# Gate tables of two expert blocks by scattered accumulating DMAs, and inverse roots on ScalarE, in a hybrid decoder block

## The chip, the cores and the metric

One core of one Trainium2 chip runs the whole kernel: one decoder layer over 1024 tokens. The metric is device time in microseconds of one launch (the slowest core, here the only one). Engine names follow the profile: PE is TensorE's matmul, PEld its weight load, DVE is VectorE, ACT is ScalarE, POOL is GpSimd, and SP issues most of the DMAs.

## The reference, cut to what matters

```python
h = rmsnorm(x, mix_norm);  zc = h @ w_in
o_dn = gated_deltanet(...)            # conv, l2norm of q and k, chunked recurrence, rmsnorm of o
o_sw = swa_sink_attention(...)        # window 128
x = x + concat(o_dn, o_sw) @ w_out
x = x + peer(rmsnorm(x, ffn_norm))    # below
gate = sigmoid(rmsnorm(x, ple_norm) @ ple_gate)
x = x + gate * (p @ ple_proj);  out = rmsnorm(x, final_norm)

def peer(h):                          # 8 heads, 128 x 128 product keys, 16384 experts
    sc = keys of both halves . query                    # (T, 8, 2, 128)
    top_s, top_i = top_k(sc, 16)
    best_s, best_pos = top_k(all 16 x 16 sums, 16)
    expert = top_i[0] * 128 + top_i[1] at best_pos      # (T, 8, 16)
    gates = softmax(best_s)
    act = gelu(h . u_tab[expert])
    return sum over heads and picks of gates * act * v_tab[expert]
```

A token picks 128 experts, 16 in each of 8 heads. The heads' picks may name the same expert; their gates then add up.

## The kernel before

The 1024 tokens are 8 blocks of 128. The work has three stages, written one behind the other; a list scheduler orders the instructions of each engine when the kernel is built, by its own times, and each engine then runs its list in order.

**Upstream** (`upstream`, from L325). `projected` multiplies p with its projection and stores the product (`pr` to the DRAM table `prd`). `project(0)` and `project(1)` each norm 4 blocks, transpose them (`hTh`, `hTl`), and multiply with w_in, first 12 column tiles `ct` (weights `wraw` from `in_wc_dram`), then the rest. Blocks then go in four groups of two: `mixers` runs DeltaNet (`deltanet`) and windowed attention (`swa`), `retrieve` the output projection (`x`, stored as `x1d`), the norm, the queries, the scores and the two top-k (`first_topk`, `topk`). `mixers(gi + 1)` stands ahead of `retrieve(gi)`, so both interleave. All matmuls of weight size are three products of high and low parts in fp32r (`mm3`).

**Gates.** Blocks 5, 6, 7 (`ABLK`) keep lists of expert numbers (`eidx`) and gates. Blocks 0 to 4 (`DBLK`) need a dense table of gates, expert by token: `topk` transposes the first and second half of each expert number and the gate into `tT`, and `gbuild` makes the table by matmul. For 4 tokens at a time DVE compares an iota with both halves (`o12`, shown as `o`), ACT scales one half by the gates, four matmuls multiply them (`bk_gm`), and ACT copies the result into `stage`; after 16 tokens SP stores 1 MB to the DRAM table `gd`:

```python
tt(o12, bc(bc(iota, 1, 4), 1, 2), bc(tT[:, 0:2, c0:c0 + 4], 3, P), ALU.is_equal)
for i in range(4):
    copy(o2[:, i], o2[:, i], scale=tT[:, 2, c0 + i:c0 + i + 1])
for i in range(4):
    mm(pg[:, i], o2[:, i], o1[:, i])
copy(stage[:, :, t0:t0 + 4], pg.rearrange("p t e -> p e t"))
```

That is 32 such steps per block, 160 in all.

**Dense** (`dense`, L918). For 128 chunks of 128 experts the hidden products of the 640 dense tokens are made in two parts of 320 columns (`bk_u`), ACT takes gelu (`ge`), DVE multiplies by the gates `Gt` loaded from `gd`, and ACT and DVE split the product in `wh` and `wl`; after each 4 chunks the products with v follow (`bk_y`, `bk_yp`). Beside it POOL gathers the rows of u and v for blocks 5 to 7 by indirect DMAs (`rows`, L852) and DVE takes dots and sums. **Final** (`final`, L1007) does the last gate and norm.

`rsqrt` (L152) is two POOL instructions, a multiply-add into `rs_v` and a power into `rs` (norms), `rq` (l2norm of q and k) or `ro` (DeltaNet's output). `swa` clears `kz` and `vz` on POOL for every block and copies v into `vz` there.

Of the kernel before, what the change touches and what calls it, by code (L numbers as in the profile page):

```python
# [6 lines left out]

# [3 lines left out]
I32 = mybir.dt.int32  # L11
# [18 lines left out]
DBLK = [0, 1, 2, 3, 4]  # L30
ABLK = [5, 6, 7]
# [14 lines left out]
def _consts():  # L46
    import numpy as np

    r = np.arange(P)
    parts = [np.eye(P), r[:, None] <= r[None, :], r[:, None] > r[None, :], np.ones((P, P)),  # L50
             np.broadcast_to(r[None, :], (P, P)), r[None, :] > r[:, None]]
    for l in range(7):
        s = 1 << l
        same = (r[:, None] // (2 * s)) == (r[None, :] // (2 * s))
        low = same & (r[:, None] % (2 * s) >= s) & (r[None, :] % (2 * s) < s)
        parts.append(low if l == 0 else low.T[:, r % (2 * s) >= s])
    sel = np.zeros((P, 8 + 50 + 16 + 16 + 16))
    sel[:, :8] = (500000.0 ** (-np.arange(0, 16, 2) / 16)).astype(np.float32)
    widths = [16 // (a + 1) for a in range(16)]
    starts = np.concatenate([[0], np.cumsum(widths)[:-1]])  # L60
    sel[:, 58:74] = starts
# [6 lines left out]
def block_kernel(ctx: ExitStack, tc, I, out, dbg=None):  # L68
# [47 lines left out]
    G.memset(mhalf, -0.5)  # L116
    early = ExitStack()
# [7 lines left out]
    negt = c2.tile([P, 1], F32, name="negt")  # L125

    def load_consts():
        nc.sync.dma_start(ident, I["consts"][:, 0:P])
        nc.sync.dma_start(cst, I["consts"][:, P:])
        V.tensor_copy(sel_b.rearrange("p s a h -> p (s a) h"), bc(sel[:, 58:106], 2, 8))  # L130
        V.memset(negt, NEG)

# [14 lines left out]
    gd = dr.tile([NE // GC, P, NT // TB, GC, TB], F32, name="gd")  # L147

    eidx = cp.tile([P, len(UBLK), P], I32, name="eidx")
    gate_a = cp.tile([P, len(UBLK), P], F32, name="gate_a")  # L150

    def rsqrt(pool, dst, src, scale, n):  # L152
        v = pool.tile([P, n], F32, tag=f"rsv{n}", name="rs_v", bufs=2)
        G.tensor_scalar(v, src, scale, EPS, op0=ALU.mult, op1=ALU.add)  # L154
        G.tensor_tensor(dst, v, mhalf[:, 0:n], ALU.pow)  # L155
# [65 lines left out]
    def project(hf, es):  # L221
# [103 lines left out]
    def upstream():  # L325
        with early as em:
# [37 lines left out]
    def mixing(dn):  # L364
        sink = row(c2, "sinks", 8)
        state = {}
# [14 lines left out]
    def retrieving(lt, es):  # L381
# [14 lines left out]
        def retrieve(gi):  # L396
# [62 lines left out]
            for bi, b in enumerate(grp):  # L459
                topk(lt, bg, b, tv[bi], tiu[bi])  # L460
                if b in HBLK:
                    pools["job"] = half_job()
                tick(2.0)

# [200 lines left out]
    def swa(dn, state, b, zc_d, cos, sin, sink, mTh, mTl, cols):  # L665
# [85 lines left out]
    def topk(tk, bg, b, v, iu):  # L751
# [52 lines left out]
        ga = gate_a[:, UBLK.index(b)] if b in UBLK else flat[:, 2 * P:3 * P]  # L804
# [9 lines left out]
        if b in ABLK:  # L814
            return
# [13 lines left out]
    slots = {}  # L829

    def gbuild(bg, b):
        tT = slots[b]
        for tb in range(P // TB):
# [13 lines left out]
            nc.sync.dma_start(gd[:, :, BBLK.index(b) * (P // TB) + tb].rearrange("g p c t -> p g (c t)"),  # L847
# [64 lines left out]
    def tick(us):  # L912
        credit[0] += us * RATE
        n = int(credit[0])
        credit[0] -= n
        advance(n)

    def dense(xB):  # L918
        with ExitStack() as es:
# [12 lines left out]
            nparts = (NU + 511) // 512  # L932
            width = (NU // nparts + TB - 1) // TB * TB
            parts = [(n0, min(width, NU - n0)) for n0 in range(0, NU, width)]
# [26 lines left out]
            for cg in range(NE // GC):  # L961
                Gt = ap.tile([P, NT // TB, GC, TB], F32, tag="Gt", name="Gt", bufs=1)
                nc.sync.dma_start(Gt, gd[cg])
                vs, ws = [], []
                for ci in range(GC):
# [10 lines left out]
                    for n0, n in parts:  # L976
# [6 lines left out]
                        g3 = ge.rearrange("p (t k) -> p t k", k=TB)  # L983
                        m0 = NH + n0
                        tt(g3, g3, Gt[:, m0 // TB:(m0 + n) // TB, ci, :], ALU.mult)
# [76 lines left out]
    upstream()  # L1062
    pools["gp"] = ctx.enter_context(tc.tile_pool(name="gp", bufs=GBUF, side="right", reuse_waits="tile"))
# [64 lines left out]
```

## Time and profile before

| | |
|---|---|
| median of 3 runs | 3049.43 us (3043.96 to 3054.33) |
| the profiled execution | 3050.88 us, of which the span from first to last instruction is 3049.1 us |
| busy, PE / DVE / ACT / POOL | 2938.0 / 2504.2 / 1234.5 / 1067.8 us |
| first matmul of the dense stage | 1124.7 us after the span's start |
| granted TensorE clock, mean | 0.984 |

Matmuls are pipelined, so a busy PE is not PE at its peak. In a row of the timeline "x3" is three instructions merged; the first number is the start, the second how long they took together.

### The profile page before, as it was taken

What the parts mean: (1) busy time and instruction counts of PE and PEld (TensorE: products, weight loads), DVE (VectorE), ACT (ScalarE), POOL (GpSimd) and SP (SyncE); (2) the same over time, 40 slices, a digit from 0 to 9 for tenths busy, and PEclk for the clock granted to TensorE, in tenths of its full rate; (3) what the DMA queues carried; (4) which work ended last, traced back from release to release, by engine and by line L of the source; (5) the groups of instructions that cost most, each with busy time, mean ns of one, the idle gap of its engine ahead of it and who ended that gap; (6) DMA issues with size and microseconds to landing.
All of it is one profiled execution on the core that took longest, in us unless ns stands there. A gap on an engine that the chain in (4) does not pass through costs nothing. (4 is left out here: it accounts for less than half of the span.)

```text
span 3049.1 us, 49772 instructions
## 1 busy us (share of the span) xinstructions
PE 2938.0 (96%) x18287; PEld 2689.7 (88%) x18287; DVE 2504.2 (82%) x5023; ACT 1234.5 (40%) x2761; POOL 1067.8 (35%) x901
## 2 busy tenths in 40 slices
PE   7999999999998879999999999999999999999998
PEld 5888999999998778989889989999899999998977
DVE  5658635998999879989799889888898898798884
ACT  5567634488777653222223223223222232222232
POOL 0000000000000002655465555555555665556531
PEclk9999999999999899999999999999999999999999
DMA  6569666689879895999899989999999898899962
GB/s 233 143 230 364 201 204 223 225 231 255 230 220 275 229 301 193 358 347 328 288 351 349 342 323 338 338 323 338 339 332 336 317 364 314 306 345 335 325 227 84
DMA packets 449812, 869.24 MB, mean 285 GB/s; under 512 B 193440, under 2 KB 235680, under 8 KB 445216
## 3 DMA queue, kind: packets, MB, share of 16 engines
q1 hardware_dynamic: 338976, 463.37, 46.3%
q0 software_dynamic: 110592, 402.70, 36.5%
q8 instruction: 143, 2.34, 0.3%
q14 instruction: 101, 0.83, 0.1%
HBM read 766.34 MB, written 99.61 MB: 284 GB/s over the span
## 5 line engine op out<-in xcount | busy, mean ns | idle before, releaser
L134 PE MATMUL bk_u<-hT,uh 128*128 128x320 f32 x4096 | 912.7, 310 | 11.9 <-DMA hT<-h2Td 8.4
L134 PEld LDWEIGHTS bk_u<-hT,uh 128*128 128x128 f32 x4096 | 693.5, 188 | 28.3 <-DMA hT<-h2Td 8.8
L852 POOL DMA_INDIRECT rows<-in_u_dram,eidx x384 | 497.6, 1296 | 553.4 <-DVE dots L862 292.4
L134 PE MATMUL bk_u<-hT,ul 128*128 128x320 f32 x2048 | 633.6, 309 | 0.0
L852 POOL DMA_INDIRECT rows<-in_v_dram,eidx x384 | 498.5, 1298 | 365.1 <-DVE acc L82 291.0
L82 DVE SCALAR_TENSOR_TENSOR acc<-rows,dots,acc 128x1024 f32<-128x1024 f32 x384 | 491.5, 1280 | 19.1 <-DMA rows<-in_v_dram,eidx 12.3
L862 DVE CUSTOM_DVE_ANT_0 rows<-rows,h2n 128x1024 f32<-128x1024 f32 x384 | 457.8, 1219 | 18.3 <-DMA rows<-in_u_dram,eidx 17.4
L982 ACT ACTIVATE ge<-bk_u 128x320 f32<-128x320 f32 x256 | 109.7, 430 | 691.0 <-PE bk_u L134 659.4
L134 PEld LDWEIGHTS bk_u<-hT,ul 128*128 128x128 f32 x2048 | 385.1, 188 | 3.7
L134 PE MATMUL bk_y<-vh,wh 128*128 128x512 f32 x768 | 299.7, 391 | 2.9 <-DVE xB L79 2.9
L134 PE MATMUL bk_y<-vl,wh 128*128 128x512 f32 x768 | 300.9, 393 | 0.0
L134 PE MATMUL bk_y<-vh,wl 128*128 128x512 f32 x768 | 299.0, 394 | 0.0
L76 ACT ACTIVATE o<-o,tT 128x128 f32<-128x128 f32 x640 | 204.0, 392 | 55.6 <-DVE o L79 54.9
L76 ACT ACTIVATE wh<-ge 128x320 fp32r<-128x320 f32 x256 | 119.0, 469 | 262.9 <-DVE ge L79 246.3
L134 PE MATMUL bk_gm<-o 128*128 128x128 f32 x1280 | 200.8, 288 | 23.3 <-ACT o L76 13.4
L76 ACT ACTIVATE uh<-ur 128x1024 fp32r<-128x1024 f32 x128 | 135.4, 1058 | 188.1 <-PE bk_u L134 177.5
L134 PE MATMUL bk_s<-h,whi 128*128 128x256 f32 x1024 | 207.2, 295 | 3.7 <-ACT sc L76 1.9
L79 DVE TENSOR_TENSOR o<-cst,tT 128x1024 f32<-128x1024 f32 x160 | 193.7, 1214 | 18.4 <-PE bk_gm L134 17.5
L134 PE MATMUL bk_yp<-vh,wh 128*128 128x512 f32 x512 | 199.4, 394 | 7.4 <-ACT wh L76 7.4
L134 PEld LDWEIGHTS bk_gm<-o 128*128 128x128 f32 x1280 | 177.6, 197 | 29.7 <-ACT o L76 17.9
L134 PE MATMUL bk_yp<-vl,wh 128*128 128x512 f32 x512 | 199.4, 394 | 0.0
L79 DVE TENSOR_TENSOR ul<-ur,uh 128x1024 fp32r<-128x1024 f32 x128 | 156.3, 1221 | 45.2 <-ACT uh L76 45.1
(302 smaller groups left out, 5805.5 us busy)
## 6 DMA issues: line engine op xcount, KB each, us to landing
ur<-in_uT_dram SPq DMA_DIRECT2D x128, 512.0 KB, 6.9
vr<-in_v_dram SPq DMA_DIRECT2D x128, 512.0 KB, 6.7
gd<-stage SPq DMA_DIRECT2D x40, 1024.0 KB, 7.4
Gt<-gd SPq DMA_DIRECT2D x32, 1280.0 KB, 9.5
wlo<-wqc SPq DMA_DIRECT2D x128, 256.0 KB, 4.5
whi<-wqc SPq DMA_DIRECT2D x128, 256.0 KB, 4.5
whi<-woc SPq DMA_DIRECT2D x64, 256.0 KB, 4.5
wlo<-woc SPq DMA_DIRECT2D x64, 256.0 KB, 4.7
```

Of the source, the lines that this page charges most:

```text
L76: return S.activation(o, i, AF.Copy, **k)
L79: return V.tensor_tensor(o, a, b, op)
L82: return V.scalar_tensor_tensor(o, a, s, b, op0, op1, **k)
L134: PE.matmul(o, l, r, start=start, stop=stop)
L852: G.indirect_dma_start(out=r, out_offset=None, in_=tab, in_offset=bass.IndirectOffsetOnAxis(ap=eidx[:, u, s:s + 1], axis=0))
L862: held_back(V.tensor_tensor_reduce(out=r, in0=r, in1=h2n, op0=ALU.mult, op1=ALU.add, scale=1.0, scalar=0.0, accum_out=dots[:, s:s + 1]))
L982: S.activation(ge, pa, AF.Gelu_apprx_tanh)
```

## The change

Blocks 0 and 1 (`SBLK`) no longer go through `gbuild`. Their gates go into a DRAM table of their own, `gsd`, of 128 x 128 experts by 256 tokens, 4 bytes each, 16.8 MB. It is zeroed by 16 DMAs of 1 MB from an SBUF tile of zeros, two in the code of each of the first eight column tiles of `project(0)`. After the top-k of both blocks, `scattered` issues 256 indirect DMAs from POOL (8 heads x 2 blocks x 16 picks); each adds one gate of each of 128 tokens to its place in `gsd`. The 16 DMAs of a head and block wait for the 16 of the head before of that block. In the dense stage `Gs` is loaded from `gsd` and serves a first part of 256 columns, `Gt` a second one of 384. From the second mixers until the dense stage `rsqrt` is two ACT instructions, Ln and Exp, in place of the two on POOL. `kz` and `vz` are three persistent pairs, cleared once, and v is copied by ACT.

```diff
+SBLK = [0, 1]
+NS = len(SBLK) * 128
...
+        V.memset(zero, 0.0)
+        for i in range(len(SBLK)):
+            V.tensor_scalar(scol[:, i:i + 1], sel[:, 8:9], float(i * P), None, op0=ALU.add)
...
+    gsd = dr.tile([NE * P * NS, 1], F32, name="gsd")
+    lanes = dram_disjoint_views(gsd, 16 * len(SBLK))
...
     def rsqrt(pool, dst, src, scale, n):
         v = pool.tile([P, n], F32, tag=f"rsv{n}", name="rs_v", bufs=2)
+        if by_log[0]:
+            S.activation(v, src, AF.Ln, scale=scale, bias=eps)
+            S.activation(dst, v, AF.Exp, scale=-0.5)
+            return
         G.tensor_scalar(v, src, scale, EPS, op0=ALU.mult, op1=ALU.add)
         G.tensor_tensor(dst, v, mhalf[:, 0:n], ALU.pow)
...
+            if not hf and ct < 8:
+                for z in range(2 * ct, 2 * ct + 2):
+                    zf = gsd.rearrange("(z p n k) o -> z p n (k o)", z=16, p=P, k=512)[z]
+                    nc.sync.dma_start(zf, bc(zero, 1, zf.shape[1]))
...
                 retrieve, half_built = retrieving(lt, es)
+                by_log[0] = True
...
+            if any(b in SBLK for b in grp):
+                scattered([b for b in grp if b in SBLK])
...
-        kz = dn.tile([P, 2, P], F32, tag="kz", name="kz", bufs=3)
-        vz = dn.tile([P, 2, P], F32, tag="vz", name="vz", bufs=3)
-        G.memset(kz, 0.0)
-        G.memset(vz, 0.0)
+        kz, vz = state["z"][b % 3]
         copy(kz[0:64, 0], pk[0:64])
         copy(kz[64:128, 1], pk[64:128])
         for kv in range(2):
-            G.tensor_copy(vz[:, kv, 64 * kv:64 * kv + 64], qk[:, 10 + kv])
+            copy(vz[:, kv, 64 * kv:64 * kv + 64], qk[:, 10 + kv])
...
-        if b in ABLK:
+        if b in SBLK:
+            si = SBLK.index(b)
+            stt(i1, i1, 128.0, i2, ALU.mult, ALU.add)
+            V.tensor_scalar(sidx[:, si], i1, float(NS), scol[:, si:si + 1], op0=ALU.mult, op1=ALU.add)
+        if b in ABLK or b in SBLK:
             return
...
+    def scattered(blocks):
+        for h in range(8):
+            for b in blocks:
+                si = SBLK.index(b)
+                now = []
+                for k in range(16):
+                    s = h * 16 + k
+                    i = G.indirect_dma_start(
+                        out=lanes[16 * si + k], out_offset=bass.IndirectOffsetOnAxis(ap=sidx[:, si, s:s + 1], axis=0),
+                        in_=sgate[:, si, s:s + 1], in_offset=None, compute_op=ALU.add)
+                    for j in sent.get(b, ()):
+                        tc.add_manual_dep(i.ins, j.name,
...
+                    now.append(i.ins)
+                sent[b] = now
...
-            parts = [(n0, min(width, NU - n0)) for n0 in range(0, NU, width)]
+            parts = [(0, NS), (NS, NU - NS)]
...
+                Gs = ap.tile([P, GC, NS], F32, tag="Gs", name="Gs", bufs=1)
+                nc.sync.dma_start(Gs, gsd.rearrange("(g c p t) o -> g p c (t o)", c=GC, p=P, t=NS)[cg])
...
+                        if n0 == 0:
+                            tt(ge, ge, Gs[:, ci], ALU.mult)
+                        else:
+                            g3 = ge.rearrange("p (t k) -> p t k", k=TB)
+                            tt(g3, g3, Gt[:, :, ci, :], ALU.mult)
...
     upstream()
+    by_log[0] = False
```

Three places show how the order of the instructions moves. SP near the program's start, before the change (`xt` are blocks of x, `prd` the stores of the first product, `wraw` raw weights):

```order
L236 DMA xt<-in_x_dram 128x1024 x2
L202 DMA wraw<-in_wp_dram 128x2x512
L182 DMA sinks<-in_sinks_dram 128x8
L202 DMA wraw<-in_wp_dram 128x2x512
L219 DMA prd<-pr 128x512 x2
L236 DMA xt<-in_x_dram 128x1024
L202 DMA wraw<-in_wc_dram 128x1024
L219 DMA prd<-pr 128x512
L236 DMA xt<-in_x_dram 128x1024
```

and now (`gsd<-zero` are the zeroing DMAs):

```order
L257 DMA xt<-in_x_dram 128x1024 x2
L223 DMA wraw<-in_wp_dram 128x2x512
L281 DMA gsd<-zero 512x1x512 x2
L223 DMA wraw<-in_wp_dram 128x2x512
L281 DMA gsd<-zero 512x1x512 x3
L240 DMA prd<-pr 128x512
L281 DMA gsd<-zero 512x1x512 x3
L240 DMA prd<-pr 128x512
L281 DMA gsd<-zero 512x1x512 x7
L257 DMA xt<-in_x_dram 128x1024
L281 DMA gsd<-zero 512x1x512
L203 DMA sinks<-in_sinks_dram 128x8
```

All 16 zeroing DMAs stand behind the second x block; 15 of them, and two of the stores, stand ahead of the third.

ACT where a DeltaNet block's q and k are normed (`sq` the sums of squares, `rq` the inverse roots, `nat` the scaled q or k), now:

```order
L564 ACTIVATE junk,sq<-qkv 128x128
L172 ACT_TABLE_LOAD
L172 ACTIVATE rs_v<-sq,eps 128x8
L173 ACT_TABLE_LOAD
L173 ACTIVATE rq<-rs_v 128x8
L80 ACTIVATE whi<-wraw 128x1024
L80 ACTIVATE nat<-qkv,rq 128x128 x4
```

Before, the squares were followed at once by other ACT work and POOL made `rq`. Of ACT_TABLE_LOAD the program had 12 and now has 52.

POOL from the last inverse roots of its own to the gathers, now:

```order
L175 TENSOR_SCALAR rs_v<-so 128x4
L176 TENSOR_TENSOR ro<-rs_v,mhalf 128x4
L869 DMA gsd<-sgate,sidx 4194304x1 x256
L901 DMA rows<-in_u_dram,eidx 128x1024 x115
```

The 256 scatters stand in one piece on POOL, ahead of every gather; each of them carries a wait for the one eight back, and the first of a head and block for all of the head before.

## Rows read from the trace of the kernel before

**Rows 1.** The page, section 1: busy time, share of the span, instructions.
```profile
PE 2938.0 (96%) x18287; PEld 2689.7 (88%) x18287; DVE 2504.2 (82%) x5023; ACT 1234.5 (40%) x2761; POOL 1067.8 (35%) x901
```
**Rows 2.** Windows: stretch, busy PE, PEld, DVE, ACT, POOL, granted clock, DMA share, GB/s.
```profile
650.00:950.00 300.00, 292.88 (x2450) 284.25 (x2449) 279.40 (x932) 229.51 (x681) 8.24 (x15) 0.99 0.86 234
950.00:1050.00 100.00, 80.33 (x558) 76.31 (x559) 85.07 (x265) 69.19 (x192) 2.78 (x4) 0.88 0.90 244
1100.00:1180.00 80.00, 57.81 (x348) 53.81 (x347) 63.40 (x295) 31.14 (x61) 4.98 (x4) 0.85 0.81 267
1250.00:2850.00 1600.00, 1596.80 (x8942) 1453.53 (x8941) 1397.40 (x1924) 425.86 (x694) 908.23 (x702) 1.00 0.91 332
```
**Rows 3.** Groups of instructions by form: the gate tables' (busy us, mean ns).
```profile
L79 DVE TENSOR_TENSOR o<-cst,tT 128x1024 f32<-128x1024 f32 x160 | 193.7, 1214 | 18.4 <-PE bk_gm L134 17.5 <-ACT tT L76 0.5
L76 ACT ACTIVATE o<-o,tT 128x128 f32<-128x128 f32 x640 | 204.0, 392 | 55.6 <-DVE o L79 54.9
L76 ACT ACTIVATE stage<-bk_gm 128x512 f32<-128x512 f32 x160 | 93.2, 588 | 43.5 <-PE bk_gm L134 42.8
L134 PE MATMUL bk_gm<-o 128*128 128x128 f32 x1280 | 200.8, 288 | 23.3 <-ACT o L76 13.4 <-ACT stage L76 9.7
```
**Rows 4.** Timeline of PE: start, time, matmul, at three places.
```profile
1103.15 1.05 PE L134 MATMUL bk_gm<-o 128*128 128x128 f32 x8
...
1099.55 0.28 PE L134 MATMUL bk_s<-h,wlo 128*128 128x256 f32 x1
1099.67 0.40 PE L134 MATMUL bk_s<-h,whi 128*128 128x256 f32 x2
1099.91 0.28 PE L134 MATMUL bk_s<-h,wlo 128*128 128x256 f32 x1
...
2000.82 0.31 PE L134 MATMUL bk_u<-hT,ul 128*128 128x320 f32 x1
2000.97 0.46 PE L134 MATMUL bk_u<-hT,uh 128*128 128x320 f32 x2
2001.26 0.31 PE L134 MATMUL bk_u<-hT,ul 128*128 128x320 f32 x1
```
**Rows 5.** Timeline of the start: SP's issue, ACT, PE.
```profile
11.36 0.38 SPq L202 DMA_DIRECT2D wraw<-in_wp_dram  x1
...
23.00 1.06 ACT L188 ACTIVATE h<-xt 128x1024 f32<-128x1024 f32 x1 [0.64 <-DMA xt<-in_x_dram]
...
52.23 0.78 PE L134 MATMUL bk_acc<-hTh,whi 128*128 128x512 f32 x1 [2.42 <-ACT pr L76]
```
**Rows 6.** Windows as in rows 2: the start, and a stretch of full DMA.
```profile
10.00:23.00 13.00, 8.13 (x31) 6.21 (x30) 9.67 (x31) 6.71 (x12) 2.48 (x4) 0.81 0.93 318
250.00:300.00 50.00, 47.01 (x297) 40.10 (x295) 42.85 (x75) 35.52 (x71) 1.50 (x4) 1.00 0.97 352
```
**Rows 7.** POOL's inverse roots (ns least/median/most); ACT's table load and a small activation.
```profile
L155 POOL TENSOR_TENSOR rs<-rs_v,mhalf x32: 548/550/1623, 16.9 to 3043.3; 128x1 f32<-128x1 f32 x32
L154 POOL TENSOR_SCALAR rs_v<-sq x8: 196/280/972, 145.8 to 741.3; 128x8 f32<-128x8 f32 x8
L155 POOL TENSOR_TENSOR rq<-rs_v,mhalf x8: 1636/1643/2082, 146.1 to 741.6; 128x8 f32<-128x8 f32 x8
...
0.73 1.28 ACT L76 ACT_TABLE_LOAD   x1 [0.73 <-PEq L1112]
...
11.65 0.20 ACT L343 ACTIVATE a_log<-a_log 128x4 f32<-128x4 f32 x1
```
**Rows 8.** The gathers on POOL (ns least/median/most), and issue to landing (us).
```profile
L852 POOL DMA_INDIRECT rows<-in_u_dram,eidx x384: 932/1242/2077, 1129.1 to 2639.9; - x192
...
  issue: 105.9, 344
...
rows<-in_u_dram,eidx POOLq DMA_INDIRECT x384, 7.0
```
**Rows 9.** Timeline: block 1's second top-k on DVE; the first gelu of the dense stage.
```profile
627.29 0.44 DVE L774 CAST pos<-pu 128x128 bf16<-128x128 uint32 x1
...
1142.64 0.44 ACT L982 ACTIVATE ge<-bk_u 128x320 f32<-128x320 f32 x1
```

More of the change, by code (lines that the diff above doesn't have):

```diff
@@ L6 @@
 from concourse._compat import with_exitstack
+from concourse.ap import dram_disjoint_views
 F32 = mybir.dt.float32
@@ L60, in _consts @@
     starts = np.concatenate([[0], np.cumsum(widths)[:-1]])
+    sel[:, 8] = r
     sel[:, 58:74] = starts
@@ L116, in block_kernel @@
     G.memset(mhalf, -0.5)
+    eps = cp.tile([P, 1], F32, name="eps")
+    G.memset(eps, EPS)
+    by_log = [False]
     early = ExitStack()
@@ L125, in block_kernel @@
     negt = c2.tile([P, 1], F32, name="negt")
+    zero = c2.tile([P, 512], F32, name="zero")
+    scol = cp.tile([P, len(SBLK)], F32, name="scol")
     def load_consts():
@@ L146, in block_kernel @@
     h2Td = [dr.tile([P, DK, NU], F32, name=f"h2Td{i}") for i in range(2)]
-    gd = dr.tile([NE // GC, P, NT // TB, GC, TB], F32, name="gd")
+    NO = NT - NS
+    gd = dr.tile([NE // GC, P, NO // TB, GC, TB], F32, name="gd")
+    gsd = dr.tile([NE * P * NS, 1], F32, name="gsd")
+    lanes = dram_disjoint_views(gsd, 16 * len(SBLK))
+    sidx = cp.tile([P, len(SBLK), P], I32, name="sidx")
+    sgate = cp.tile([P, len(SBLK), P], F32, name="sgate")
     eidx = cp.tile([P, len(UBLK), P], I32, name="eidx")
@@ L365, in mixing @@
         sink = row(c2, "sinks", 8)
-        state = {}
+        state = {"z": [[c2.tile([P, 2, P], F32, name=f"{n}{i}") for n in ("kz", "vz")] for i in range(3)]}
+        for z in state["z"]:
+            for t in z:
+                G.memset(t, 0.0)
         dn_state = [c2.tile([P, 4, P], F32, name=f"dnS{i}") for i in range(2)]
@@ L460, in retrieve @@
                 topk(lt, bg, b, tv[bi], tiu[bi])
-                if b in HBLK:
-                    pools["job"] = half_job()
                 tick(2.0)
+            if any(b in SBLK for b in grp):
+                scattered([b for b in grp if b in SBLK])
         def half_built():
@@ L802, in topk @@
             tick(7.5)
-        ga = gate_a[:, UBLK.index(b)] if b in UBLK else flat[:, 2 * P:3 * P]
+        ga = gate_a[:, UBLK.index(b)] if b in UBLK else sgate[:, SBLK.index(b)] if b in SBLK else flat[:, 2 * P:3 * P]
         gv = ga.rearrange("p (h k) -> p h k", k=16)
@@ L829, in block_kernel @@
     slots = {}
+    sent = {}
+    def scattered(blocks):
[10 more added lines that the diff above has]
+                        tc.add_manual_dep(i.ins, j.name,
+                                          mybir.DependencyInfo(mybir.DependencyClass.Sync, mybir.DependencyReason.DATA),
+                                          reason="one head behind another")
+                    now.append(i.ins)
+                sent[b] = now
     def gbuild(bg, b):
@@ L846, in gbuild @@
                 yield
-            nc.sync.dma_start(gd[:, :, BBLK.index(b) * (P // TB) + tb].rearrange("g p c t -> p g (c t)"),
+            nc.sync.dma_start(gd[:, :, (BBLK.index(b) - len(SBLK)) * (P // TB) + tb].rearrange("g p c t -> p g (c t)"),
                               stage.rearrange("p (g c) t -> p g (c t)", c=GC))
@@ L931, in dense @@
             nc.sync.dma_start(xB, x1d[BBLK[0]:BBLK[0] + NB].rearrange("b p d -> p b d"))
-            nparts = (NU + 511) // 512
-            width = (NU // nparts + TB - 1) // TB * TB
-            parts = [(n0, min(width, NU - n0)) for n0 in range(0, NU, width)]
+            parts = [(0, NS), (NS, NU - NS)]
             total = len(ABLK) * 2 * P
@@ L961, in dense @@
             for cg in range(NE // GC):
-                Gt = ap.tile([P, NT // TB, GC, TB], F32, tag="Gt", name="Gt", bufs=1)
+                Gt = ap.tile([P, NO // TB, GC, TB], F32, tag="Gt", name="Gt", bufs=1)
                 nc.sync.dma_start(Gt, gd[cg])
+                Gs = ap.tile([P, GC, NS], F32, tag="Gs", name="Gs", bufs=1)
+                nc.sync.dma_start(Gs, gsd.rearrange("(g c p t) o -> g p c (t o)", c=GC, p=P, t=NS)[cg])
                 vs, ws = [], []
@@ L982, in dense @@
                         S.activation(ge, pa, AF.Gelu_apprx_tanh)
-                        g3 = ge.rearrange("p (t k) -> p t k", k=TB)
-                        m0 = NH + n0
-                        tt(g3, g3, Gt[:, m0 // TB:(m0 + n) // TB, ci, :], ALU.mult)
+                        m0 = n0
+                        if n0 == 0:
[3 more added lines that the diff above has]
+                            tt(g3, g3, Gt[:, :, ci, :], ALU.mult)
                         copy(wh[:, m0:m0 + n], ge)
```

## The prediction

> **What bounds the kernel now.** I read the page's busy times first: PE is busy for 96% of the span, DVE for 82% [rows 1]. Since a busy PE can still be waiting, I then read the windows by stage [rows 2]. From 1250 to 2850 us, the dense stage, PE is busy for 1596.80 of 1600 us at a granted clock of 1.00: that stage lasts as long as its matmuls, and nothing that only takes work from DVE, ACT or POOL there is worth anything. From 650 to 950 PE is busy for 292.88 of 300 and DVE for 279.40: PE leads, with DVE close behind. From 950 to 1050 PE drops to 80.33 of 100 while DVE stays at 85.07, and from 1100 to 1180, where the dense stage starts up, PE has 57.81 of 80. So PE is short of work by about 20 + 22 = 42 us in these two tails, and the time before 950 is shortened only by work taken off PE. A gain must come out of the upstream stage, and a delay at the program's start is paid in full, because everything behind it is bound by PE.
>
> **What the change removes.** Of the 160 steps that build gate tables, 64 go. Each is one DVE compare of 1214 ns, four ACT scalings of 392 and one ACT copy of 588 ns [rows 3]: DVE loses 64 x 1.214 = 78 us and ACT 64 x 2.156 = 138 us. PE loses 256 matmuls. Their mean of 288 ns is latency, the pace is read from the timeline: eight in 1.05 us, so (1.05 - 0.28) / 7 = 0.11 us each [rows 4], 256 x 0.11 = 28 us, 29 with the six transposes of `tT`. While PE leads, at about 97% busy, this is worth **30 us**. The DVE time counts where DVE holds PE up, in the tails: at most the 42 us. I take 27, nearer the upper end, since the work that DVE loses is just what it has queued there; the start-up's loads of the dense stage remain. Bounds: 0 and 42.
>
> **What it adds at the start.** The zeroing DMAs look as if spread over eight column tiles, but the order puts all 16 directly behind the second block of x. They carry 16.8 MB, and 15.7 MB stand ahead of the third block. The DMA engines are not free there: from 10 to 23 us they are busy for 0.93 [rows 6]. At full load they moved 352 GB/s with a share of 0.97, so 363 GB/s at most, and 15.7 MB take 43 us. The queue reaches them at 11.36; before, the third block had landed by 23.00 [rows 5], and in these 12 us a free share of 0.07 gives back 1 us. So the third block lands about 42 us later. What follows it, up to the first matmul of a column tile at 52.23 [rows 5], hangs on it: norm, transposes, and twelve more products whose stores stand behind it on SP. Two of those products and a weight tile can be ready ahead, some 4 us. I take **+38 us**, with bounds of 10 (if the zeros pass in the gaps of the queue) and 46 (all 16, nothing given back). PE has nothing else to do there, and later stages have no slack to take it up.
>
> **What it adds on ACT.** 20 inverse roots become Ln and Exp, and the order shows a table load ahead of each: 40 more loads of 1.28 us [rows 7], 51 us of ACT. ACT loses 138 us in the same stage, so it is not the bound; but a pair holds it for 2 x 1.28 + 2 x 0.20 = 2.97 us, where POOL took 0.28 + 1.64 = 1.92 for `rq` beside ACT [rows 7]. Copies that feed PE wait behind the pair. Bounds: 0 and 51 us; PE interleaves three streams of work there, so I take **+8**. The copies of v, 16 short ones, go with these. POOL's clears of `kz` and `vz` delayed nobody on the path and go for nothing.
>
> The Trainium skill, "ScalarE: Activation LUTs", section "What ACT_TABLE_LOAD costs", counts the drain as well, 2.66 us a switch; by it the 40 loads would hold ACT for 106 us in place of 51. Its section on table sets says that one set holds ln and exp, so that Ln followed by Exp needs one load; the order of this program shows two.
>
> **What it adds on POOL.** The 256 scatters are new; their price is not in this trace. The nearest rows are the gathers, also 128 indices each: 0.93 us at the least, 1.24 in the median, 2.08 at the most, with 106 us of issue gaps over 344 of them, 0.3 each [rows 8]. I take 1.24 + 0.3 = 1.54 us. The indices of block 1 exist about 17 us behind its cast at 627.29 [rows 9], so the scatters start near 627 + 17 + 38 - 7 = 675 (7 us is DVE work of block 0's table that stood ahead) and end at 675 + 256 x 1.54 = 1069. The dense stage needs `Gs` at its first gelu, before at 1142.64 [rows 9], now near 1143 + 38 - 57 + 8 = 1132. So 63 us are to spare and the cost is 0. The break-even is (1132 - 675) / 256 = **1.79 us** a scatter; at 2.08 the table is ready at 1207, 75 us late. No other POOL work waits behind them until the gathers, since the inverse roots and clears have left.
>
> **What it moves in the dense stage.** A pair of 320-column parts becomes 256 and 384. Three matmuls of 256 columns take 0.36 us and three of 320 take 0.44 [rows 4], so 0.120 and 0.147 each; on that line 384 takes 0.174, and 0.120 + 0.174 = 0.294 is twice 0.147: **0**. `Gt` and `Gs` together carry the bytes of the old `Gt`; if they come late by a few microseconds PE has the products with v to do.
>
> **Sum**, against the profiled execution's own 3050.88 us (1.5 over the median shown, 3049.43): + 38 - 30 - 27 + 8 + 0 + 0 = -11, so **3040 us**, 0.36% less. A measurement of this kernel tells 0.3%, 9 us, from no change. It is a small difference of larger terms: with start and tails each some 15 us off and tables between 0 and 20 this case alone spans 3015 to 3065.
>
> **Rivals.**
> 1. *The scatters outlive the upstream stage* (slower; 0.18). The place is the first `ge` times `Gs`; PE has two PSUM banks for `bk_u` and stops after them. It decides from 1.79 us a scatter, or from a landing beyond 8 x 1.79 = 14 us, as each waits for the one eight back. For it: each sum must fetch the old value first, and the slowest gather took 2.08. Against: gathers of 4 KB rows land in 7.0 us, and these move 4 bytes. At 2.08: 3040 + 75 = 3115. The Trainium skill, "DMA: Bandwidth & Descriptors", section on the anatomy of one DMA, gives a fixed 2.0 us each; paid one after the other it would be 512 us, past the limit, but the order keeps eight in flight.
> 2. *ACT's table loads stand in the chain* (slower; 0.14). If PE waits out every pair, 51 us in place of 8: 3083. For it: X, scores and queries all leave PSUM through ACT. Against: the 138 us that ACT loses.
> 3. *The zeros cost little* (faster; 0.12). If they slip into gaps, or the work behind catches up, 10 in place of 38: 3012. Against: the 0.93 above.
> 4. *The tails do not shrink* (0.10): the dense start waits for the same loads, and 4-byte packets crowd out weight loads. 27 becomes 0: 3067.
>
> My forecast has 0.46. **How the numbers follow.** The forecast splits into 0.25 faster by over 0.3%, 0.13 within, 0.08 slower; rival 1 into 0.02, 0.02, 0.14; rival 2 into 0.03, 0.04, 0.07; rival 3 is 0.12 faster; rival 4 is 0.03 within and 0.07 slower. Together 0.42 faster, 0.22 the same, 0.36 slower. The range runs from 3000, between the forecast's own lower end of 3015 and what all kind bounds together would give (3050.88 + 10 - 30 - 42 + 0 = 2989), to 3110, just short of rival 1's price; it leaves out the late end of rival 1 and the deepest gains.
>
> **What would show it.** Right: in the new profile the third block of x reaches ACT near 65 us with DMA share near 1 from 12 on; the first matmul of a column tile is near 90; the first dense matmul is near 1125 - 11 = 1114; the last scatter is issued before it; the stretch behind 1250 is as full as before. Wrong at the start if that first column tile stands below 70; wrong on tables if PE's gaps from 450 to 950 end on ACT and exceed those of now by over 20 us; wrong on the scatters if DVE waits on `Gs` or the last one is issued past 1110.

## The result and the profile after

| | before | changed |
|---|---|---|
| median of 4 runs each, us | 3046.69 (3041.70 to 3054.33) | 3137.82 (3133.42 to 3143.07) |
| ratio, 95% interval | | 1.0294 [1.0277, 1.0311] |
| span of the profiled execution, us | 3049.1 | 3135.8 |

The change costs 91 us; I had forecast a gain of 11, and 3137.82 lies beyond my range. The page's busy times of the changed kernel answer to [rows 1]:

```profile
PE 2907.1 (93%) x17769; PEld 2647.7 (84%) x17769; DVE 2441.5 (78%) x4966; ACT 1187.2 (38%) x2535; POOL 1474.9 (47%) x1092
```

The work that was to go is gone (518 recorded matmuls, 63 us of DVE, 47 of ACT), yet PE's share falls from 96% to 93%: the span grew by waiting. (ACT's 47 is what is left after the new roots and copies are added.) The windows say where. The first two rows are the start, the next three answer to [rows 2], the sixth is the hole behind the upstream stage, the last the dense stage. The columns are those of [rows 2]:

```profile
0.00:50.00 50.00, 17.85 (x52) 12.28 (x52) 17.44 (x50) 14.14 (x21) 4.29 (x16) 0.72 0.97 363
50.00:100.00 50.00, 24.41 (x87) 17.87 (x88) 13.85 (x13) 18.10 (x29) 2.96 (x8) 0.70 0.84 283
650.00:950.00 300.00, 275.24 (x2196) 263.13 (x2195) 248.46 (x943) 182.34 (x508) 231.75 (x135) 0.97 0.84 203
950.00:1050.00 100.00, 79.39 (x602) 75.23 (x600) 93.41 (x350) 72.13 (x196) 86.39 (x45) 0.96 1.10 263
1100.00:1180.00 80.00, 53.87 (x401) 51.99 (x399) 35.53 (x140) 26.58 (x69) 67.19 (x43) 0.88 0.91 223
1150.00:1200.00 50.00, 17.10 (x126) 16.90 (x124) 2.34 (x3) 3.12 (x6) 41.52 (x27) 0.72 0.39 57
1250.00:2850.00 1600.00, 1593.90 (x8928) 1450.74 (x8929) 1413.92 (x2104) 428.67 (x696) 892.79 (x688) 1.00 0.90 328
```

In the first 100 us PE works 42 us; the kernel before had 81.03 there. From 650 to 950 it is no longer full, and from 1150 to 1200 PE has 17 us of work, DVE and ACT next to none, while POOL goes on. The dense stage runs as before (8928 matmuls in that stretch, 8942 before). The granted clock fell too where PE had little to do: 0.72 and 0.70 in the first two windows and 0.72 in the hole, where the kernel before had 0.90, 0.97 and 0.90. How much of the loss is the clock's I did not separate. What POOL does at 1150 is seen in the view of the tile `gsd` (count, ns least/median/most, first and last start), and what POOL's idle time before it ended on:

```profile
L869 POOL DMA_INDIRECT gsd<-sgate,sidx x256: 1547/1550/3772, 675.2 to 1197.9; - x128
L1012 SPq DMA_DIRECT2D Gs<-gsd x32: 371/378/752, 1201.1 to 2924.4; - x32
L281 SPq DMA_DIRECT2D gsd<-zero x16: 752/1625/2641, 12.2 to 53.0; - x16
...
  DVE sidx L843: 251.8, 1
  issue: 77.1, 253
```

The scatters start at 675.2, but one follows the other every (1197.9 - 675.2) / 255 = 2.05 us, beyond the break-even of 1.79, and `Gs` is first loaded at 1201.1. The waits from 950 to 1300, and from 0 to 100 (total us, times, longest):

```profile
DVE ge L83 <- DMA Gs<-gsd: 42.1, 1, 42.1
PEld bk_s L146 <- DMA whi<-wqc: 41.4, 3, 40.2
```
```profile
DVE h L86 <- POOL rs L176: 42.0, 5, 37.2
...
PE bk_tp L149 <- DVE h L86: 25.8, 2, 21.5
ACT h L209 <- DMA xt<-in_x_dram: 25.3, 4, 20.9
```

DVE waits 42 us for the gates of blocks 0 and 1, PE as long for query weights (one wait of 40, whose loads stand behind `Gs` on SP), and at the start the chain hangs on a block of x. So there are three suspects: the zeros, the scatters' end, and, since the change also put table loads on ACT, ln and exp.

### The profile page after: what moved, and what is told of

The parts are those of the page before. It is cut to its first block, busy times and chain, and to the rows that moved or that the text cites. A ratio compares the mean times of both kernels' runs of the same rounds, so it can differ in the third digit from the quotient of the medians.

```text
span 3135.8 us, 48710 instructions
## 1 busy us (share of the span) xinstructions
PE 2907.1 (93%) x17769; PEld 2647.7 (84%) x17769; DVE 2441.5 (78%) x4966; ACT 1187.2 (38%) x2535; POOL 1474.9 (47%) x1092
## 5 line engine op out<-in xcount | busy, mean ns | idle before, releaser
L146 PE MATMUL bk_u<-hT,uh 128*128 128x256 f32 (+1 forms) x4096 | 905.3, 310 | 12.6 <-DMA hT<-h2Td 11.6
L146 PE MATMUL bk_u<-hT,ul 128*128 128x256 f32 (+1 forms) x2048 | 634.0, 310 | 0.8 <-DVE ul L83 0.8
L869 POOL DMA_INDIRECT gsd<-sgate,sidx x256 | 444.5, 1736 | 331.5 <-DVE sidx L843 251.8
L1031 ACT ACTIVATE ge<-bk_u 128x256 f32<-128x256 f32 (+1 forms) x256 | 109.4, 430 | 485.8 <-PE bk_u L146 452.4
L80 ACT ACTIVATE wh<-ge 128x384 fp32r<-128x384 f32 (+1 forms) x256 | 118.5, 469 | 374.2 <-DVE ge L83 339.0
L146 PEld LDWEIGHTS bk_s<-h,whi 128*128 128x128 f32 x1024 | 162.5, 193 | 50.1 <-DMA whi<-wqc 45.1
L80 ACT ACTIVATE vh<-vr 128x1024 fp32r<-128x1024 f32 x128 | 131.7, 1053 | 178.6 <-PE bk_y L146 118.9
L83 DVE TENSOR_TENSOR xB<-bk_y,xB 128x512 f32<-128x512 f32 x192 | 130.8, 689 | 85.1 <-PE bk_y L146 84.9
```

The lines of the kernel that those rows point to most:

```text
L80: return S.activation(o, i, AF.Copy, **k)
L83: return V.tensor_tensor(o, a, b, op)
L146: PE.matmul(o, l, r, start=start, stop=stop)
L869: i = G.indirect_dma_start(out=lanes[16 * si + k], out_offset=bass.IndirectOffsetOnAxis(ap=sidx[:, si, s:s + 1], axis=0), in_=sgate[:, si, ...
L1031: S.activation(ge, pa, AF.Gelu_apprx_tanh)
```

## The experiments

All times are medians, all ratios against the kernel before on the same chip; the edits are shortened. My first theory was that three costs (start, SP's queue behind `Gs`, table loads) add up to the 91 us and what the removal gains.

**Zeros out of SP's start** (ratio 1.0124 [1.0107, 1.0141]).
```diff
-            if not hf and ct < 8:
-                for z in range(2 * ct, 2 * ct + 2): nc.sync.dma_start(zf[z], zero)
+            rc = copy(raw[:, 3:], pc)
+            z = 12 * hf + ct
+            if z < 16: S.dma_start(zf[z], zero)   # dependent on rc
```


> The changed kernel, but the 16 zeroing DMAs leave SP's queue: each is issued by ACT behind the first copy of one column tile, 12 in the first half of the blocks and 4 in the second, so none stands ahead of the third x block. Theory (the zeros cost the start about 42 us, which is passed on unshortened to the end): the third x block is there near 24 us again, the first column tile near 52, project's, retrieve's and the scatters' marks all move 40 earlier (scatters from about 633 to 1156), and the time falls from 3138 to about 3096. Rival (the same 16 MB only delay the weights of the column tiles instead): the column tiles stretch by what the start gains, and the time stays within 3125 to 3140.


3089.61 us, 48 back. Its windows of the start are those of the kernel before again (33.27 and 47.77 there), though the same 16 MB now flow from 60 to 240 us:
```profile
0.00:50.00 50.00, 34.19 (x128) 25.42 (x128) 28.60 (x61) 28.89 (x47) 7.25 (x24) 0.90 0.85 289
50.00:100.00 50.00, 48.31 (x211) 39.07 (x212) 31.27 (x49) 25.75 (x37) 0.00 (x0) 0.97 0.79 258
```
The theory holds for the start: what cost was the place of the zeros, not their bytes.

**The wait for the scatters: not waiting, half of them, `Gs` off SP.**
```diff
-                nc.sync.dma_start(Gs, gsd...[cg])
+                nc.sync.dma_start(Gs, gd[cg]...[:, 0:GC * NS])           # e2
+                (G if cg == 0 else nc.sync).dma_start(Gs, gsd...[cg])    # e4
-        for h in range(8):
+        for h in range(4):                                              # e3
```


> The changed kernel with all 256 scatters, but the Gs tiles are read from the other gate table (the same bytes, 512 KB each), so nothing waits for the scatters; the gates of blocks 0 and 1 are therefore not used in the output. Theory (the loss behind 1100 us is a wait: Gs's load stands in SP's queue until the last scatter has landed near 1200, and the query weights behind it stand too, PE idle): the stretch 1150:1200 gets from 17 to over 42 us of matmuls, and the time falls by 60 to 70 us, to about 3073. Rival (the scatters' packets and POOL's work themselves slow the loads and VectorE): the time stays above 3115.

> The changed kernel with the scatters of heads 0 to 3 alone, 128 of 256; half the gates of blocks 0 and 1 are left out. The 128 end near 675+128x2.05=937, well ahead of Gs. Theory (a wait for the last scatter): as without the wait, about 3073, within 8 us of it. Rival (contention by the scatters between 675 and 1200): half of it stays until 937 and none behind, so that it is over 15 us faster than the run in which all scatters go but nothing waits.

> The changed kernel, but the first Gs tile is loaded by POOL, behind its scatters, and no longer by SP. Theory that SP's in-order queue does the damage (query weights standing behind Gs, 40 us of PE waits): PE keeps its query matmuls, only the first gate product waits until about 1215, and 35 to 45 us come back, to about 3097. Rival (the wait for the gates is what costs, wherever it stands: PE can run only two u banks ahead of the first gate product): PE idles as long behind that product, and the time stays within 3125 to 3140.


Not waiting: 3096.14 us, 42 back; half the scatters: 3090.81, 47 back, though their last starts at 940.2. From 1150 to 1200 PE has 45.80 and 49.18 us of work. The wait is real, with 42 to 47 us smaller than the 60 to 70 expected. (Half the scatters also take half of whatever else scatters cost; that adds 5 us here, within the noise.) But `Gs` off SP gives 3135.80, nothing. Its waits from 950 to 1300:
```profile
DVE ge L83 <- DMA Gs<-gsd: 44.6, 1, 44.6
PEld bk_u L146 <- ACT ge L1031: 38.6, 2, 38.1
```
The query weights flow now and PE stops on the next thing, the banks of `bk_u` that nobody empties. My reading of SP's queue fell; it is the gates themselves that are late.

**Ln and exp.** First alone in the kernel before, then with a copy in place of ln (no loads).
```diff
-        G.tensor_scalar(v, src, scale, EPS, op0=ALU.mult, op1=ALU.add)
-        G.tensor_tensor(dst, v, mhalf[:, 0:n], ALU.pow)
+        S.activation(v, src, AF.Ln, scale=scale, bias=eps)   # e5; e12: AF.Copy, scale=scale
+        S.activation(dst, v, AF.Exp, scale=-0.5)
```


> The kernel before with one part of the change alone: the inverse roots by ACT's ln and exp from the second mixers on; no table of zeros, no scatters, swa as before. Theory (in the changed kernel some 20 us are lost between 417 and 513 whatever the start does, and they are the table loads of ln and exp in the chain): some 40 table loads more, x1d of blocks 0 and 1 stored near 470 where the kernel before has 452, and the time 20 to 50 us over the kernel before, about 3075. Rival (they lie beside other work; the loss at 417 to 513 is another order of the work, or swa's zeros and copies): within 10 us of 3049.

> The kernel before with the roots on ACT as two instructions, but the first is a scaled copy in place of ln, so that no table is loaded for them (the roots' values, exp(-v/2) for v^(-1/2), are not the reference's; the work has the same instructions and sizes). Theory that the table loads are the price (some 40 x 1.28 us in the chain of the norms): within 8 us of 3049. Rival (a root in ACT's in-order queue waits behind other ACT work, as it would behind VectorE's, where POOL answered at once): 30 to 48 us above, 3080 or more.


Ln and exp: 3096.91 us, 1.0156 [1.0134, 1.0177], 48 slower. Without loads: 3076.02, 1.0095 [1.0077, 1.0112], still 29 slower. By these two times alone, the 40 loads would be only some 20 of the 48. The traces say otherwise. Here are the dense stage's products `bk_u` that are done by 1300 us (PE's busy time in them, and their number) in the kernel before, without loads, and with ln and exp:
```profile
0.00:1300.00 1300.00, 90.62 (x576) 87.97 (x576) 10.39 (x24) 0.97 0.78 243
0.00:1300.00 1300.00, 91.35 (x577) 88.47 (x578) 10.26 (x24) 0.97 0.77 237
0.00:1300.00 1300.00, 72.14 (x460) 70.21 (x461) 8.00 (x19) 0.96 0.77 237
```
All roots on ACT lie ahead of this point, the last near 1051 us. Without loads the run is level there with the kernel before; with them it is 116 products behind, an estimate of 34 us at the 0.29 us that a product takes in the dense stage (1500 us for 5154). So most of the 48 are the loads, and a root on ACT without a load cost PE nothing that is seen here. (Each trace is of one execution; that of the run without loads is its fastest, 3071.47.) The second run loses its 29 us later, most of them from 1350 to 2850 us, in which the kernel before does 5154 products and this run 75 fewer:
```profile
1350.00:2850.00 1500.00, 787.87 (x5154) 772.16 (x5155) 91.52 (x214) 1.00 0.91 332
1350.00:2850.00 1500.00, 778.75 (x5079) 761.93 (x5080) 90.95 (x211) 1.00 0.91 331
```
Its roots have other values, so its picks differ and it gathers other rows; whether that slows its dense stage is not shown. How a root stands in the chain shows the timeline of ACT in the changed kernel:
```profile
512.66 1.28 ACT L172 ACT_TABLE_LOAD   x1
513.95 0.30 ACT L172 ACTIVATE rs_v<-so,eps 128x4 f32<-128x4 f32 x1
514.27 1.28 ACT L173 ACT_TABLE_LOAD   x1
515.56 0.20 ACT L173 ACTIVATE ro<-rs_v 128x4 f32<-128x4 f32 x1
```
From the first load to the end of the root 3.1 us pass, and whatever needs the root waits for them. The Trainium skill, "ScalarE: Activation LUTs", section "What ACT_TABLE_LOAD costs", counts 2.66 us a switch with the drain; here no row shows more than the 1.28.

**Roots elsewhere**: on POOL again (`by_log` never set), or by VectorE (a seed by shift and subtraction, three Newton steps).


> The changed kernel with the inverse roots of all blocks by POOL's power again, so that they share POOL's in-order queue with the 256 scatters (in runs of up to 96 between two groups of roots). Theory: the loads of tables go (52 to 12), and retrieve of blocks 0 and 1 gets its 20 us back, but from 675 on a root stands behind up to 96x2.05=197 us of scatters and the mixers and norms wait for it: slower than the changed kernel by 100 us or more, above 3240. Rival (roots wait little, since the mixers have time to spare): 20 to 40 us faster than the changed kernel, near 3105.

> The changed kernel, but the inverse roots that it gives to ACT are made by VectorE alone (a seed by shift and subtraction, three Newton steps: 12 small instructions a root, no table load, nothing on POOL). Some 22 groups of roots x 12 x about 0.08 us is 21 us more of VectorE, partly beside other work. Theory (the table loads cost the changed kernel what they cost the kernel before, 48 us, whole): 3138-48+0..21, so 3090 to 3111. Rival (the costs overlap: what is lost behind 675 us lies beside the scatters, which the dense stage waits for anyway, so only the 20 us lost ahead of the scatters' start come back): 3113 to 3123, with the last scatter near 1178 instead of 1198.


On POOL: 3346.62 us, 1.0971 [1.0947, 1.0995]. The waits from 640 to 1300 name it:
```profile
DVE zs L86 <- POOL ro L176: 153.5, 4, 138.5
PEld bk_dn L149 <- DVE zs L86: 145.8, 2, 136.6
```
One `ro` stood behind scatters for 138.5 us: with 256 scatters on POOL the roots had to leave it. By VectorE: 3137.38, no gain, although 40 loads are gone. The last scatter starts at 1183.6 there and not at 1197.9, so a little was won ahead of it; what takes it back is not shown (that the 12 instructions a root sit in another busy queue is a guess).

**Both edits, and an earlier start of the scatters** (one head of block 0 ahead).


> The changed kernel with both edits: zeroing DMAs by ACT behind the column tiles, inverse roots by VectorE. If the terms add up (48 for the start, 48 less 0 to 21 for the roots): 3042 to 3063. If only what is lost ahead of the scatters' start counts (48 and 20): 3065 to 3078, PE still idle for some 40 us or more behind 1085 until the last scatter near 1135.

> Both edits (zeros spread, roots by VectorE) with both blocks by scatters, and the scatters of block 0's first head issued before block 1's picks are done, then a head of either block in turn: the first starts some 45 us earlier, the last ends some 30 us earlier (the two heads that go alone wait for their own landings). If the dense stage waits for the last scatter, the time follows by 30 us: 3035 to 3045. If the scatters no longer end last by then: the same as without, within 8 us.


3080.67 us (1.0092) and 3086.68 (1.0125). The second edit moved nothing: its first scatter starts at 610.7, without it at 611.2, since the first 16 belonged to block 0 before too. It tells nothing of the wait.

**One block by scatters**, a search for a version that beats both, all three with the zeros spread: parts of 128 and 512 columns; parts of 256 and 384 with roots by VectorE; the same with roots on POOL and the scatters strewn between them.


> The changed kernel with two edits: only block 0 goes by scatters (128 scatters, a table of 8 MB, block 1 built on TensorE again), and the zeroing DMAs are issued by ACT behind the column tiles. By the two terms measured so far, which take 48 (start) and 42 to 47 us (wait for the scatters) off 3138: 3043 to 3048, less nothing, plus about 15 for the 128 one-hot matmuls and the copies and subtractions of block 1 that come back, so 3050 to 3065. If the two terms overlap, 3085 or more.

> The run before this one with block 0 alone by scatters (128 of them, over near 890; block 1 built on TensorE), and the columns of the dense stage still split 256 and 384, the first part's product in two pieces. By the accounting (no cost of the start, no wait for the scatters, no table loads, half of the 57 us that I expected of the removed work): 3049-28=3021, plus 0 to 21 for VectorE's roots: 3021 to 3045. If the 215 us by which the one-block run with parts of 128 and 512 was slower than its forecast did not come from the 128-column matmuls: above 3100.

> Block 0 alone by scatters, columns split 256 and 384, zeros spread, and the roots on POOL again, with the 128 scatters strewn between them: each scatter stands behind an instruction of VectorE that is issued some 1.5 us of work after the one before, so that POOL meets runs of 3 to 39 scatters between two groups of roots instead of 128. If a root waits only a few us and half of the 57 us for the removed work shows: 3025 to 3045, faster than both kernels. If the roots wait behind the longer runs (39 x 2.05 = 80 us) or VectorE bounds the stretch anyway: 3050 to 3090.


3214.92 us (1.0546), 3097.72 (1.0154), 3091.25 (1.0140). The first was bound by a cost that I had not counted. PE's timeline in its dense stage (start, time, number), a part of 128 columns and one of 512, each from one group of three matmuls to the next; then the 384 columns of the changed kernel:
```profile
2004.36 0.38 PE L146 MATMUL bk_u<-hT,uh 128*128 128x128 f32 x2
2004.58 0.28 PE L146 MATMUL bk_u<-hT,ul 128*128 128x128 f32 x1
2004.69 0.39 PE L146 MATMUL bk_u<-hT,uh 128*128 128x128 f32 x2
...
2007.46 0.62 PE L146 MATMUL bk_u<-hT,uh 128*128 128x512 f32 x2
2007.92 0.39 PE L146 MATMUL bk_u<-hT,ul 128*128 128x512 f32 x1
2008.15 0.62 PE L146 MATMUL bk_u<-hT,uh 128*128 128x512 f32 x2
```
```profile
2011.10 0.51 PE L146 MATMUL bk_u<-hT,uh 128*128 128x384 f32 x2
2011.45 0.34 PE L146 MATMUL bk_u<-hT,ul 128*128 128x384 f32 x1
2011.63 0.51 PE L146 MATMUL bk_u<-hT,uh 128*128 128x384 f32 x2
```
Three matmuls of 128 columns take 0.33 us where three of 256 take 0.36 [rows 4]: halving the width saves next to nothing. Three of 512 take 0.69 and three of 384 take 0.53, so a group costs 1.02 us in place of 0.89. Over 128 chunks with 8 groups each that is some 130 us, an estimate, and most of the 150 to 165 us by which this run missed its forecast. The other two are 44 to 49 us slower than the kernel before, without zeros in the start and with their last scatter at 902 and 1004; how that splits I did not settle. No version that I ran with its full work beats the kernel before.

**The rest of the account.** Two edits without the wait, with ln and exp and without loads:
```diff
+ zeros by ACT (e1), Gs from the other table (e2)                        # e14
+ the same, AF.Copy in place of AF.Ln                                    # e13
```


> As the run with three costs out, but with ln and exp and their table loads (the gates of blocks 0 and 1 are not used). If the start and the wait add up: 3138-48-42..47 = 3043 to 3048. If they overlap (an earlier start only lengthens another wait): 3060 or more. What it stands above the run with three costs out is the price of the table loads in the changed kernel: near 48 if it is what the kernel before pays.

> The changed kernel without any of the three suspected costs: zeroing DMAs by ACT behind the column tiles, Gs read from the other gate table (the gates of blocks 0 and 1 are not used), roots by a scaled copy and exp (no table loads, values not the reference's). All 256 scatters still run. If the costs add up (48, 42 to 47, and up to 48) and the removed one-hot work is worth what I expected of it (30+27): 3138-138..143 = 2995 to 3000. If the costs overlap, or the removed work only uncovers another limit (VectorE's top-k, which stands at 93 to 97 of 100 us between 600 and 1000 in the kernel before): 3025 or above.


With ln and exp: 3059.89 us (1.0037 [1.0023, 1.0052]): start and wait give 78 back together, 12 less than apart. The other, 3346.79, is no measure of the loads. POOL waited for its own scatters, which the changed kernel does for 2.3 us in all:
```profile
POOL gsd L872 <- DMA gsd<-sgate,sidx: 141.5, 45, 19.0
```
Its roots have other values and so other picks; that these fall on the same rows and collide is argued, not shown. So I left the scatters out (and with them the gates of blocks 0 and 1), with zeros spread, and put back the roots, then swa:
```diff
-                scattered([b for b in grp if b in SBLK])
+                pass                                     # e16 with roots on POOL, e17 with ln and exp
-        kz, vz = state["z"][b % 3]
+        kz, vz = dn.tile(...), dn.tile(...)              # e18: e16, cleared and copied by POOL
```


> The changed kernel without a single scatter (the gates of blocks 0 and 1 are left out and stay zero), zeroing DMAs spread behind the column tiles, roots on POOL as in the kernel before. What is left of the change is the removed one-hot work, the zeroing beside the column tiles, Gs's loads and swa's copies on ACT. If the removed work is worth the 57 us of the prediction: 3047-57=2990, give or take 8. If only what the runs so far leave for it (48+30+48-91=35): 3012. If VectorE's picks bound the stretch: 3035 or above.

> The same with ln and exp on ACT. Above the run with the roots on POOL by the price of ln and exp in the changed kernel: 48 if it is what the kernel before pays, under 15 if it lies beside other work here. Against 3060 of the run in which 256 scatters go and nobody waits for them: within 5 us if scatters cost nothing but their waiting, 15 us or more below if they slow the other engines.

> The run without scatters and with the roots on POOL, and swa's clears and copies of v on POOL again as in the kernel before (the gates of blocks 0 and 1 are left out). If the copies on ACT cost the 19 us: x1d of blocks 0 and 1 near 452, and the time 10 to 19 us below 3018, near 3003. If the 19 us are another order of PE's work between 380 and 470, or the zeroing DMAs' traffic up to 240: within 8 us of 3018, x1d of blocks 0 and 1 wherever that order puts it.


3018.39 us (0.9913 [0.9890, 0.9937]), 3036.21 (0.9960 [0.9948, 0.9973]) and 2997.61 (0.9833 [0.9815, 0.9851]). These make a ladder, each rung one edit more, each against its own runs of the kernel before (on the fourth, `Gs` also comes from the other gate table):

| rung | us over before | step |
|---|---|---|
| removed work alone (zeros spread, no scatters) | -52 | -52 |
| swa's clears once, its copies on ACT | -29 | +23 |
| ln and exp | -11 | +18 |
| 256 scatters that nobody waits for | +13 | +24 |
| waiting for the last of them | +40 | +27 |
| zeros in the start | +91 | +51 |

The steps add up to 91 because the ladder is built that way. A step is uncertain by some 5 to 9 us (its two ratios' intervals together). The last two depend on their order: with the zeros still in the start, not waiting stands at +47, so the wait is worth 44 and the zeros 34. Each step also holds the edit together with the order that the planner makes of it: all of PE's order upstream shifts with any of them. Where a step falls can be read as before, from the `bk_u` products done by 1300 us, here of the four lowest rungs in turn:
```profile
0.00:1300.00 1300.00, 121.33 (x773) 118.27 (x773) 13.82 (x32) 0.97 0.78 252
0.00:1300.00 1300.00, 122.04 (x768) 117.80 (x768) 13.81 (x32) 0.96 0.77 249
0.00:1300.00 1300.00, 105.82 (x670) 102.42 (x670) 11.59 (x27) 0.96 0.76 242
0.00:1300.00 1300.00, 104.08 (x652) 99.58 (x653) 11.44 (x27) 0.96 0.82 240
```
By 1300 us, at 0.29 us a product, swa's edit has cost 1 us, ln and exp 28 (10 of which the end does not show) and the scatters 5. The rest of swa's 23 and of the scatters' 24 comes later, where neither swa nor a scatter runs. For swa it is seen from 1350 to 2850 us, where the run without its edit does 5179 products and the one with it 5113:
```profile
1350.00:2850.00 1500.00, 797.02 (x5179) 782.75 (x5180) 92.10 (x215) 1.00 0.92 334
1350.00:2850.00 1500.00, 782.84 (x5113) 768.69 (x5114) 90.89 (x213) 1.00 0.92 333
```
So the step of 23 is not shown to be a cost of swa's; why the dense stage runs at another pace is open. The mark that made me suspect it, x1d of blocks 0 and 1 stored 19 us late (470.8 against 451.6), is at 479.0 with swa put back: it was another order, and no cost of swa's. For the scatters' 24 there is this, windows from 900 to 1000 with and without them:
```profile
900.00:1000.00 100.00, 84.02 (x641) 81.05 (x641) 85.69 (x283) 71.09 (x198) 85.97 (x47) 0.94 1.10 249
```
```profile
900.00:1000.00 100.00, 85.00 (x632) 81.62 (x630) 85.45 (x284) 70.64 (x189) 0.00 (x0) 0.91 0.90 260
```
The DMA share is 1.10 against 0.90 and the engines move less, 249 against 260 GB/s; but PE is as busy in both, so this shows no loss of PE's. One thing more reaches behind the upstream stage: POOL issues its first gather at 1231.7 us in the changed kernel and at 1129.1 before, as the scatters stand ahead of it. By the views of the tiles `rows` and `bk_y`, the end comes 120 and 118 us behind the last gather, but 128 and 114 us behind the last product with v, now and before. That the late gathers cost these 14 us I did not test.

## Why the prediction was wrong

- **Removed work, -30 and -27: the sum right, its parts not.** The lowest rung is -52. But I multiplied the 256 matmuls of the code by the pace of recorded ones, and each of the code's is recorded twice: [rows 3] has 1280 for 160 steps, and the changed kernel has this row, so 512 are gone, at 0.11 us each 56 us and not 28:
```profile
L146 PE MATMUL bk_gm<-o 128*128 128x128 f32 x768 | 126.7, 303 | 30.4 <-ACT o L80 26.7 <-ACT stage L80 3.6
```
  That alone is about the -52, so the tails' 27 did not come on top. The windows up to the moment when 600 of the dense stage's products are done show it, of the kernel before and of the lowest rung:
```profile
0.00:1307.70 1307.70, 1215.69 (x8768) 1132.61 (x8769) 1016.62 (x3023) 765.14 (x1993) 128.38 (x159) 0.97 0.78 244
0.00:1244.90 1244.90, 1156.55 (x8239) 1074.28 (x8240) 926.85 (x2927) 656.82 (x1670) 106.00 (x141) 0.97 0.77 247
```
  The lowest rung is there 63 us sooner: PE is busy for 59 us less and idle for 4 us less (88 in place of 92). So the matmuls' term was half of what it should have been, and the tails, which I put at 27, shrank by 4. Two errors met in a sum that fits; that was luck.
- **Scatters, 0: the step that failed.** I took 1.24 + 0.3 us from the gathers' median and found 63 us to spare. The tile's view has 1.55 in the median, but the mean, which sets the end, is 1.74, and 2.05 with the gap:
```profile
L869 POOL DMA_INDIRECT gsd<-sgate,sidx x256 | 444.5, 1736 | 331.5 <-DVE sidx L843 251.8
```
  So the table is ready near 1200 and not at 1069, and DVE waits 42 us for it. A time of 2.05 lay inside my bound of 2.08, and rival 1 named place, break-even and end (1207, measured 1198 to 1201). Rival 1 is what happened; I gave it 0.18. Its price was wrong the other way: 75 us by arithmetic, 27 to 47 in runs. That PE still had query products and two banks to fill would explain it, but is not shown. What I had not counted at all is the 24 us between no scatters and scatters that nobody waits for, whose cause is open. My start of 675 was met by chance: block 1's picks came 63 us later than before (`pos` at 690.0, not 627.29), 32 later than I had allowed, but the first 16 scatters belong to block 0. Of the 102 us between forecast and measurement, 51 are the scatters' by the ladder (27 and 24), 23 swa's step, 13 the zeros, 10 ACT and 5 the removed work.
- **Zeros, +38: right in kind.** They cost 48 to 51, above my upper bound of 46, where the scatters are waited for, and 34, give or take 8, where they are not: the size depends on what else waits. The third block of x reached ACT at 63.36 (forecast 65), the first column tile began at 95.85 (forecast 90): from the third block to the tile it took 32 us and not 25. Rival 3, which put the zeros at 10, fell.
- **ACT, +8: too small.** Ln and exp cost 18 here and 48 in the kernel before. I set ACT's lost 138 us against the loads, but a load that stands in the chain of a root delays what needs the root, however idle ACT is otherwise: in the kernel before 34 us are lost by 1300 us and 48 in the whole, of the loads' own 51, and without loads nothing is lost by then. This is rival 2 in part; its 51 is nearly met in the kernel before, not here.
- **Swa's clears and copies, nothing: open.** Their rung is 23 us, but only 1 of it falls by 1300 us, so the runs do not show that the clears and copies are what costs. I had put the copies into ACT's term by their count and the clears at nothing, with no row for either.
- **Dense split, 0: right.** The stretch from 1250 is as full as before, 1593.90 against 1596.80, with as many matmuls.

The signs that I had set were the right ones: DVE does wait on `Gs`, the last scatter goes out past 1110, and the first dense matmul is at 1135.30, not 1114. The sign for the tables stayed just silent: from 450 to 950 PE is idle for 34.6 us against 16.0 before, and I had asked for over 20 more. With the ladder's steps, -52 + 23 + 18 + 24 + 27 + 51 = +91.

## What to carry to other kernels

When hundreds of one new instruction stand in a row, take a price that no row shows as a range and not as the median of a cousin: half a microsecond times 256 was twice the margin of 63 us. Where a small operation moves to another engine, price what stands in its chain there, not only that engine's busy share: 20 roots cost 48 us on ACT, near the 51 us of their 40 table loads, though ACT was busy for some 40% of the span. When an experiment has other values than the original, look where in the trace its time differs before reading its total. And bytes that nobody needs early belong behind work that paces them, not ahead of the first loads: the same 16 MB cost 34 to 51 us in one place and nothing that the start's windows show in the other.

## What I had not expected of the hardware

- An accumulating scatter of 128 numbers of 4 bytes holds POOL longer (1.55 us at the median, 1.74 in the mean, 3.77 at the most) than a gather of 128 rows of 4 KB (1.24 and 2.08 [rows 8]). The Trainium skill, "DMA: Bandwidth & Descriptors", section on the anatomy of one DMA, has a fixed 2.0 us each; the trace's 2.05 from one to the next is near it, but is POOL's own 1.74 and a gap of 0.3, and not a landing.
- The two loads a pair of ln and exp stand in the trace throughout (20 at ln and 18 at exp in the changed kernel), though by the Trainium skill, "ScalarE: Activation LUTs", section "Table sets: the hidden batching unit", one set holds both functions.
- Three fp32r matmuls of 128 columns take 0.33 us of PE's timeline, and three of 256 columns take 0.36.
- The dense stage's pace can differ at nearly the same busy share: PE is busy for 1497.63 and 1490.74 of the 1500 us from 1350 to 2850 in the two lowest rungs, 7 us apart, and does 5179 and 5113 `bk_u` products, an estimate of 19 us apart.
